# Attention with a bias on one core: reordering the first loads, the first scores and the bias slots

## The chip, the core and the metric

The kernel runs on one core of a Trainium2 chip. The time is the device time of the launch in microseconds (us), the median of several executions. An execution counts as slow when it is over 1.5% above the fastest of the same kernel. A profile, here also called a look, is of one execution. Its span leaves some of the launch out (250.02 us of time had a span of 247.9 us), so spans are compared with spans and times with times. PE is the matmul engine, ACT the one that computes exponentials, DVE the one for elementwise work, POOL the one that issues the loads which convert from f32 to bf16.

## The reference

```
scores = q @ k^T / sqrt(64) + bias          # q, k, v: 4 x 8 x 1024 x 64; bias: 1 x 1 x 1024 x 1024
attn   = exp(scores - max) / (sum(exp(scores - max)) + 1e-8)
out    = attn @ v                            # float32
```

## The kernel before

The 32 heads are worked on in 16 pairs. Scores stand in PSUM with the keys on partitions. The work is cut into 512 banks of 128 keys by 512 queries, three to a *slot*: PE fills a slot's PSUM tile, ACT takes its exponential. There are two such tiles, so a slot's scores can start only when the exponential of the slot two before has ended. exp(bias) is multiplied in afterwards by DVE. It is computed once, in four *bias slots* that use the same PSUM tiles: PE transposes a part of the bias (16 transposes), ACT takes the exponential.

```python
    def s_fill(g):                       # scores of slot g
        ps = ps_s.tile([P, 3, HQ], F32, tag="s", name="ps")
        ...
            nc.tensor.matmul(ps[:, j, :], kT[:, kc, :], qT[:, h, qh * HQ:(qh + 1) * HQ], ...)      # L129
    def s_exp(g):
        nc.scalar.activation(e_at(...), open_ps.pop(("S", g))[:, :n, :], ACTF.Exp, scale=scale)    # L136
    def b_fill(qh, k0):                  # a bias slot: 16 transposes, L144; its exponential is L149
        ps = ps_s.tile([P, 3, 2 * HQ], BF, tag="s", name="pb")...
    ...
        load_qk(1)                       # k and q of pair 1: among the first loads
    ...
        dummy(P)                         # a matmul on zeros, to keep PE busy
        s_fill(0)
        s_exp(0)
        pk1 = k_trans(2, 2, "xa")        # k chunks 2 and 3 of pair 0
        s_fill(1)
        nc.vector.tensor_copy(kT0[:, 2:QC, :], pk1[:])
        nc.vector.memset(vall[:, :, :, D:D1], 1.0)
        s_exp(1)
        pk2 = k_trans(QC, QC, "xb")
        s_fill(2)
        nc.vector.tensor_copy(kT0[:, QC:, :], pk2[:])
        s_exp(2)
        load_v(0)
        nc.gpsimd.dma_start(out=btraw[:, QC:, :], in_=bf_[:, QC:, :])      # second half of the bias
        load_v(1)
        load_qk(2)
```

From slot 3 on the order of every engine's instructions comes from a small simulation when the program is built. It knows a cost for each kind of work (constants such as `MUL = 600` ns) and the times at which loads are expected (`bias_at`, `raw_at`). The result is a fixed order: if PE's next instruction waits, PE waits. The places of the bias slots among the others are set by hand. Transposes of later pairs ("pieces", L89) go through one of two small PSUM buffers, from which DVE copies them (L102 for k, L98 for q).

The softmax here doesn't subtract the row's maximum and nothing guards it: scores larger than these inputs give would overflow.

Of the kernel before, what the change touches and what calls it, by code (L numbers as in the profile page):

```python
# [15 lines left out]
def kernel(  # L16
# [17 lines left out]
    P = 128  # L34
# [37 lines left out]
    def load_qk(pr):  # L72
        qr = raw.tile([P, 2, NCH, D], BF, name="qr")
        kr = raw.tile([P, 2, NCH, D], BF, name="kr")
        nc.gpsimd.dma_start(out=kr.rearrange("p t c d -> p t (c d)"), in_=kf[pr])  # L75
        nc.gpsimd.dma_start(out=qr.rearrange("p t c d -> p t (c d)"), in_=qf[pr])  # L76
        raws[pr] = (qr, kr)

    def load_v(pr):
        for t in range(2):  # L80
            nc.gpsimd.dma_start(out=vall[:, 2 * pr + t, :, :D], in_=vf[pr, :, t])  # L81
# [34 lines left out]
    def e_at(b, n):  # L116
        if b // ET not in etiles:
            etiles[b // ET] = ep.tile([P, ET, HQ], BF, name="E")
        return etiles[b // ET][:, b % ET:b % ET + n, :]
# [3 lines left out]
    def s_fill(g):  # L123
        ps = ps_s.tile([P, 3, HQ], F32, tag="s", name="ps")
        open_ps[("S", g)] = ps
        for j, b in enumerate(slots[g]):
            pr, h, qh, kc = banks[b]
            qT, kT = trs[(pr, 0)], trs[(pr, 1)]
            nc.tensor.matmul(ps[:, j, :], kT[:, kc, :], qT[:, h, qh * HQ:(qh + 1) * HQ],  # L129
                             start=True, stop=b not in late_bias)  # L130
            if b in late_bias:
                nc.tensor.matmul(ps[:, j, :], ident[:], braw[:, late_bias[b], :], start=False, stop=True)

    def s_exp(g):
        n = len(slots[g])
        nc.scalar.activation(e_at(slots[g][0], n), open_ps.pop(("S", g))[:, :n, :], ACTF.Exp, scale=scale)  # L136
# [14 lines left out]
    def mul_pair(b, n=2):  # L151
        pr, h, qh, kc = banks[b]
        e = e_at(b, n)
        if n == 1 or banks[b + 1][1] == h:
            nc.vector.tensor_tensor(e, e, eb[:, qh, kc:kc + n, :], op=ALU.mult)  # L155
        elif n == 4:
            e = e.rearrange("p (c t) q -> p c t q", t=2)
            nc.vector.tensor_tensor(e, e, eb[:, qh, kc:kc + 2, :].unsqueeze(2).to_broadcast([P, 2, 2, HQ]),  # L158
                                    op=ALU.mult)
        else:  # L160
            nc.vector.tensor_tensor(e, e, eb[:, qh, kc:kc + 1, :].to_broadcast([P, n, HQ]), op=ALU.mult)  # L161
# [76 lines left out]
    with tc.manual_schedule():  # L238
# [21 lines left out]
        for x in range(2):  # L260
            for y in range(2):
                nc.vector.memset(mask[x * D:(x + 1) * D, y, :], 1.0 if x == y else 0.0)
        load_qk(1)

        wm = ps_s.tile([P, 3, HQ], F32, tag="s", name="wm")

        def dummy(n):
            nc.tensor.matmul(wm[:, 0, :n], zeros[:, :P], zeros[:, :n], start=True, stop=True)  # L268
# [5 lines left out]
        def k_trans(c0, n, tag):  # L274
            px = ps_x.tile([P, n, P], BF, tag=tag, name="px")
            for c in range(n):
                for t in range(2):
                    nc.tensor.transpose(px[t * D:(t + 1) * D, c, :], kr0[:, t, c0 + c, :], ident[:])
            return px
# [18 lines left out]
            "p b (c q) -> p (b c) q", q=P)[:, :QC, :])  # L298
        q_out(1, pq1)
        nc.scalar.copy(kr0[:, :, 2:QC, :], k0f[:, :, 2:, :])  # L300
        dummy(P)
        s_fill(0)
        s_exp(0)
        pk1 = k_trans(2, 2, "xa")
        s_fill(1)
        nc.vector.tensor_copy(kT0[:, 2:QC, :], pk1[:])
        nc.vector.memset(vall[:, :, :, D:D1], 1.0)
        s_exp(1)
# [3 lines left out]
        s_exp(2)  # L312
        load_v(0)
        nc.gpsimd.dma_start(out=btraw[:, QC:, :], in_=bf_[:, QC:, :])
        load_v(1)
        load_qk(2)

# [3 lines left out]
        EXP, EXP0, QK, AV, TP = 427, 45, 216, 170, 350  # L321
        MUL, COPYQ, COPYK, EVAC, SEM = 600, 650, 420, 620, 80
        order = [("S", g) for g in range(3, NS)]
        for at, x in ((4, (0, 0)), (6, (0, 4)), (10, (1, 0)), (12, (1, 4))):
            order.insert(at, ("B",) + x)
        NO = len(order)
        T0 = 7000.0
        t_act, t_pe, t_dve = T0 + 1400, T0, T0 + 300
        filled = []
        act_end = []  # L330
        x_free = {"xa": T0 - 500, "xb": T0 + 200}
        x_unit = {}
        bias_at = [13000, 21500]
        raw_at = {0: (5900, 7000), 1: (15500, 16500), 2: (26000, 28500)}
        pieces = [(0, 0, 1)]
        for pr in range(1, NP):
            pieces += [(pr, 1, 0), (pr, 0, 0), (pr, 1, 1), (pr, 0, 1)]
# [1 line left out]
        pieces.append((NP, 0, 0))  # L339
        raw_at[NP] = (T0, T0)  # L340
        piece_end = {(0, 1, 0): T0, (0, 0, 0): T0, (0, 1, 1): T0 + 200}
        eb_at = {}
        exp_at = {x: T0 + (0 if x < 3 else 1400) for x in range(6)}
        mul_at = {}
# [14 lines left out]
        ends = {NB - 6: 1, NB - 5: 2, NB - 3: 1}  # L359

        def pe_cost(t, c):
            return c * 2 if t < COLD else c
# [5 lines left out]
        def act_end_of(i):  # L368
            if i < 0:
                return T0  # L370
            if i < len(act_end):
# [162 lines left out]
        def dve_pick():  # L534
            nonlocal mul_next
            c = list(dve_q)
            if mul_next < NB and mul_next not in late_bias:
                pr, h, qh, kc = banks[mul_next]
                b = mul_next
                n = ends.get(b, 2)  # L540
                if b + n - 1 in exp_at and (qh, kc) in eb_at:
                    ready = max(exp_at[b + n - 1], eb_at[(qh, kc)]) + SEM

                    if n == 2 and b % 4 == 0 and b + 3 in exp_at and (qh, kc + 1) in eb_at and b + 3 not in late_bias and \
                            exp_at[b + 3] + SEM <= max(t_dve, ready) and \
                            all(x[0] > max(t_dve, ready) + MUL for x in dve_q):
                        n = 4
                    cost = MUL * n // 2 - 70 * (n // 4)

                    def run(t):  # L550
                        nonlocal mul_next
                        mul_pair(b, n)
                        for x in range(n):
                            mul_at[b + x] = t + cost
                        mul_next += n
                    c.append((ready, 2, cost, run))
            if not c:
                return None
            return min(c, key=lambda x: (max(x[0], t_dve + 100), x[1]))
# [7 lines left out]
        while len(act_end) < NO or av_next < NA or any(last_left) or dve_q:  # L567
            c = []
            a, d, p = act_pick(), dve_pick(), pe_pick()
            if a:  # L570
                c.append((a[0], 0))
# [8 lines left out]
            if who == 0:  # L580
                i = a[2]
                item = order[i]
                t_act = t + a[1]
# [11 lines left out]
            elif who == 1:  # L595
                if d in dve_q:
                    dve_q.remove(d)
                t_dve = t + d[2]
                d[3](t)
            else:  # L600
                t_pe = t + pe_cost(t, p[1])
# [31 lines left out]
```

## Time and profile before

| | before |
|---|---|
| time, median | 250.89 us (3 runs), later 250.74 (6 runs, 250.30 to 251.31) |
| span of the profile | 248.6 us |
| slot 2's exponential starts | 8.37 us |
| second bias half lands | 23.03 us |
| third bias exponential starts | 24.32 us |
| ACT's last exponential ends | 243.83 us |

The third row marks where ACT's row begins to be full, the last where it ends; after it come 4.7 us of last matmuls, division and store. The lines behind this table stand in the prediction.

### The profile page before, as it was taken

What the parts mean: (1) busy time and instruction counts of PE and PEld (TensorE: products, weight loads), DVE (VectorE), ACT (ScalarE), POOL (GpSimd) and SP (SyncE); (2) the same over time, 40 slices, a digit from 0 to 9 for tenths busy, and PEclk for the clock granted to TensorE, in tenths of its full rate; (3) what the DMA queues carried; (4) which work ended last, traced back from release to release, by engine and by line L of the source; (5) the groups of instructions that cost most, each with busy time, mean ns of one, the idle gap of its engine ahead of it and who ended that gap; (6) DMA issues with size and microseconds to landing.
All of it is one profiled execution on the core that took longest, in us unless ns stands there. A gap on an engine that the chain in (4) does not pass through costs nothing.

```text
span 248.6 us, 7122 instructions
## 1 busy us (share of the span) xinstructions
PE 227.5 (92%) x3098; PEld 141.5 (57%) x3153; DVE 219.1 (88%) x377; ACT 240.0 (97%) x183; POOL 53.6 (22%) x74
## 2 busy tenths in 40 slices
PE   7778899999999999999999999999999999999893
PEld 3255656555666656656556556566565555665552
DVE  5228899999999999999999999999999999998884
ACT  4899999999999999999999999999999999999993
POOL 8652413360130221302213055016000000000000
PEclk9999999999999999999999999999999999999998
DMA  5999999599193493921925769629911102020111
GB/s 115 193 197 190 192 132 147 55 148 165 45 154 61 87 119 85 98 87 27 181 44 97 83 87 176 80 87 111 110 38 42 46 0 88 3 84 3 48 60 65
DMA packets 48175, 23.79 MB, mean 96 GB/s; under 512 B 34448, under 2 KB 44048, under 8 KB 47888
## 3 DMA queue, kind: packets, MB, share of 16 engines
q0 software_dynamic: 42272, 14.42, 53.7%
q1 hardware_dynamic: 5584, 8.72, 9.8%
q8 instruction: 24, 0.39, 0.6%
q10 hardware_dynamic: 288, 0.20, 0.3%
q14 instruction: 7, 0.06, 0.1%
HBM read 29.36 MB, written 8.39 MB: 152 GB/s over the span
## 4 chain that ended last, share of the span: by engine, by line
ACT 73%; PE 13%; DMA 5%; DVE 5%; issue 2%; POOL 1%; ACTq 0%
ACT E L136 71%; PE ps L129 8%; DMA btraw<-in_bias_dram 5%; PE px L89 2%; ACT eb L149 1%; PE po L186 1%; DVE E L155 1%; PE wm L268 1%; DVE E L161 1%; DVE E L158 1%; POOL vall L81 1%; DVE qT L98 1%; PE pb L144 0%; PE po L219 0%; DVE oall L198 0%
## 5 line engine op out<-in xcount | busy, mean ns | idle before, releaser
L136 ACT ACTIVATE E<-ps 128x1536 bf16<-128x1536 f32 (+2 forms) x172 | 230.1, 1682 | 1.5 <-PE ps L129 1.4
L129 PE MATMUL ps<-qT,kT 128*128 128x512 bf16 x457 | 135.2, 379 | 12.1 <-ACT E L136 5.4
L186 PEld LDWEIGHTS <-E 128*128 128x128 bf16 x2016 | 82.0, 97 | 37.6 <-DVE E L158 1.6
L158 DVE TENSOR_TENSOR E<-E,eb 128x2048 bf16<-128x2048 bf16 x82 | 98.8, 1216 | 1.1 <-ACT E L136 0.7
L186 PE MATMUL po<-vall,E 128*128 128x65 bf16 x2016 | 91.4, 194 | 1.2 <-DVE E L158 0.5
L129 PEld LDWEIGHTS <-kT 128*128 128x128 bf16 x512 | 45.3, 96 | 43.3 <-issue 8.6
L161 DVE TENSOR_TENSOR E<-E,eb 128x1024 bf16<-128x1024 bf16 x84 | 55.7, 683 | 6.3 <-ACT eb L149 5.2
L75 POOL DMA_DIRECT2D kr<-in_k_dram x15 | 10.5, 700 | 94.6 <-PE px L89 92.7
L81 POOL DMA_DIRECT2D vall<-in_v_dram x32 | 28.1, 883 | 6.6 <-DMA btraw<-in_bias_dram 4.2
L198 DVE TENSOR_TENSOR oall<-po,rs 128x256 f32<-128x256 f32 x63 | 26.7, 424 | 2.3
L98 DVE TENSOR_TENSOR qT<-px,mask 128x1024 bf16<-128x1024 bf16 x31 | 21.3, 687 | 5.6 <-PE px L89 5.0
L102 DVE COPY kT<-px 128x512 bf16<-128x512 bf16 x30 | 12.6, 421 | 2.4 <-PE px L89 1.9
L76 POOL DMA_DIRECT2D qr<-in_q_dram x15 | 10.8, 717 | 18.1 <-PE px L89 16.8
L196 DVE RECIPROCAL rs<-po 128x4 f32<-128x4 f32 x63 | 11.1, 177 | 3.8 <-PE po L186 3.3
L89 PE MATMUL px<-ident,qr 128*64 128x128 bf16 x248 | 12.8, 225 | 0.1
L89 PE MATMUL px<-ident,kr 128*64 128x128 bf16 x240 | 12.4, 225 | 0.3 <-DVE oall L198 0.3
L89 PEld LDWEIGHTS <-qr 128*64 128x64 bf16 x248 | 7.8, 109 | 8.3 <-issue 7.2
L89 PEld LDWEIGHTS <-kr 128*64 128x64 bf16 x240 | 7.7, 109 | 6.3 <-issue 4.6
L149 ACT ACTIVATE eb<-pb 128x2048 bf16<-128x2048 bf16 x4 | 7.5, 1879 | 0.2 <-PE pb L144 0.2
L144 PE MATMUL pb<-ident,btraw 128*128 128x128 bf16 x64 | 4.6, 226 | 1.9 <-ACT eb L149 0.8
L144 PEld LDWEIGHTS <-btraw 128*128 128x128 bf16 x64 | 4.5, 147 | 2.5 <-issue 1.3
L155 DVE TENSOR_TENSOR E<-E,eb 128x1024 bf16<-128x1024 bf16 (+2 forms) x7 | 4.6, 686 | 0.2 <-ACT E L136 0.2
(44 smaller groups left out, 25.8 us busy)
## 6 DMA issues: line engine op xcount, KB each, us to landing
out_dram<-oall SPq DMA_DIRECT2D x30, 256.0 KB, 2.1
vall<-in_v_dram POOLq DMA_DIRECT2D x32, 128.0 KB, 6.6
kr<-in_k_dram POOLq DMA_DIRECT2D x15, 256.0 KB, 4.0
qr<-in_q_dram POOLq DMA_DIRECT2D x15, 256.0 KB, 6.0
btraw<-in_bias_dram POOLq DMA_DIRECT2D x2, 1024.0 KB, 11.3
out_dram<-oall SPq DMA_DIRECT2D x3, 128.0 KB, 1.7
k0f<-in_k_dram SPq DMA_DIRECT2D x2, 128.0 KB, 2.9
q0f<-in_q_dram ACTq DMA_DIRECT2D x1, 128.0 KB, 2.6
```

What stands on the lines that cost most here:

```text
L76: nc.gpsimd.dma_start(out=qr.rearrange("p t c d -> p t (c d)"), in_=qf[pr])
L81: nc.gpsimd.dma_start(out=vall[:, 2 * pr + t, :, :D], in_=vf[pr, :, t])
L89: nc.tensor.transpose(px[t * D:(t + 1) * D, c, :], src[:, t, half * QC + c, :], ident[:])
L98: nc.vector.tensor_tensor(dst[:, :, half * HQ:(half + 1) * HQ], px.rearrange("p c q -> p (c q)").unsqueeze(1).to_broadcast([P, 2, HQ]), ma ...
L102: nc.vector.tensor_copy(dst[:, half * QC:(half + 1) * QC, :], px[:])
L129: nc.tensor.matmul(ps[:, j, :], kT[:, kc, :], qT[:, h, qh * HQ:(qh + 1) * HQ], start=True, stop=b not in late_bias)
L136: nc.scalar.activation(e_at(slots[g][0], n), open_ps.pop(("S", g))[:, :n, :], ACTF.Exp, scale=scale)
L158: nc.vector.tensor_tensor(e, e, eb[:, qh, kc:kc + 2, :].unsqueeze(2).to_broadcast([P, 2, 2, HQ]), op=ALU.mult)
L161: nc.vector.tensor_tensor(e, e, eb[:, qh, kc:kc + 1, :].to_broadcast([P, n, HQ]), op=ALU.mult)
L186: nc.tensor.matmul(acc[:, i, :], e[:, 0, i * P:(i + 1) * P], vall[:, 2 * pr + h, kc, :], start=(kc == 0 and i == 0), stop=(kc == NCH - 1), ...
L196: nc.vector.reciprocal(rs[:], acc[:, :, D:D1])
L198: nc.vector.tensor_tensor(oall[:, c0:c0 + QC, :], acc[:, :, :D], rs[:].to_broadcast([P, QC, D]), op=ALU.mult)
```

## The change

The aim is to have the second bias half on the chip before its slot is due, by loading it and pair 0's V ahead of pair 1's k and q. Pair 1's pieces then come later, so both late bias slots move one place earlier, ahead of pair 1's first slot (slot 11). At the start, slot 1's scores go ahead of four k transposes and a dummy matmul goes. The numbers of the simulation follow.

```diff
-        load_qk(1)                                  # from among the first loads ...
-        dummy(P)
         s_fill(0)
         s_exp(0)
+        s_fill(1)
         pk1 = k_trans(2, 2, "xa")
-        s_fill(1)
...
         nc.gpsimd.dma_start(out=btraw[:, QC:, :], in_=bf_[:, QC:, :])
+        load_qk(1)                                  # ... to behind the second bias half
         load_v(1)
...
-        for at, x in ((4, (0, 0)), (6, (0, 4)), (10, (1, 0)), (12, (1, 4))):
+        for at, x in ((4, (0, 0)), (6, (0, 4)), (9, (1, 0)), (11, (1, 4))):
...
-        T0 = 7000.0
+        T0 = 8000.0                                 # and the starting times that hang on it
-        bias_at = [13000, 21500]
-        raw_at = {0: (5900, 7000), 1: (15500, 16500), 2: (26000, 28500)}
+        bias_at = [13300, 20800]
+        raw_at = {0: (5900, 7800), 1: (22200, 23500), 2: (26000, 28500)}
...
                     cost = MUL * n // 2 - 70 * (n // 4)
+                    if b in ends:
+                        cost = 420 if n == 1 else 690
```

More of the change, by code (lines that the diff above doesn't have):

```diff
@@ L323 @@
         order = [("S", g) for g in range(3, NS)]
-        for at, x in ((4, (0, 0)), (6, (0, 4)), (10, (1, 0)), (12, (1, 4))):
+        for at, x in ((4, (0, 0)), (6, (0, 4)), (9, (1, 0)), (11, (1, 4))):
             order.insert(at, ("B",) + x)
         NO = len(order)
-        T0 = 7000.0
-        t_act, t_pe, t_dve = T0 + 1400, T0, T0 + 300
+        T0 = 8000.0
+        t_act, t_pe, t_dve = T0 + 1400, T0 + 200, T0 + 100
         filled = []
         act_end = []
-        x_free = {"xa": T0 - 500, "xb": T0 + 200}
+        x_free = {"xa": T0 - 500, "xb": T0 + 100}
         x_unit = {}
-        bias_at = [13000, 21500]
-        raw_at = {0: (5900, 7000), 1: (15500, 16500), 2: (26000, 28500)}
+        bias_at = [13300, 20800]
+        raw_at = {0: (5900, 7800), 1: (22200, 23500), 2: (26000, 28500)}
         pieces = [(0, 0, 1)]
```

## The prediction

> **What bounds the kernel now.** I read the page's busy shares first. ACT (ScalarE), which does every exponential, is busy 97% of the span, PE 92% and DVE 88%. Three shares this close decide nothing, so I cut the span at two moments in the timeline: where ACT's third exponential starts (8.37 us) and where its last one ends (243.83 us).
>
> ```profile
> PE 227.5 (92%) x3098; PEld 141.5 (57%) x3153; DVE 219.1 (88%) x377; ACT 240.0 (97%) x183; POOL 53.6 (22%) x74
> ...
> 5.92:8.37 2.45, 2.45 (x18) 0.85 (x19) 0.89 (x3) 1.62 (x2) 0.40 (x2) 1.00 1.17 189
> 8.37:243.83 235.46, 219.67 (x3039) 137.84 (x3094) 213.78 (x359) 235.25 (x174) 48.04 (x61) 1.00 0.65 95
> 243.83:248.60 4.77, 0.86 (x26) 0.73 (x24) 1.20 (x6) 0.52 (x3) 0.00 (x0) 0.75 0.18 57
> ```
>
> The row of a stretch gives its limits, its length, then the busy time of PE, weight loads, DVE, ACT, POOL. In the middle stretch ACT is busy 235.25 of 235.46 us: the time is 8.37 us of start, one unbroken queue of exponentials, and 4.77 us of end. Nothing that PE, DVE or a DMA does in the middle can shorten it, except by removing ACT's idle time. So the next view is what ACT waits for between 5 and 246 us.
>
> ```profile
> ACT E L136 <- PE ps L129: 1.4, 2, 0.7
> ACT oh L232 <- DVE rh L228: 0.8, 1, 0.8
> ACT eb L149 <- PE pb L144: 0.2, 1, 0.2
> ```
>
> Columns: total, times, longest. Two waits of together 1.4 us for the first scores, one of 0.2 us for a bias transpose (L144), and one in the closing stretch. The chain of waits shows what is behind the 0.2 us: the second half of the bias, which lands at 23.03.
>
> ```profile
> 8.03 1.76 POOL vall L81 x2
> 9.79 13.24 DMA btraw<-in_bias_dram
> 23.03 0.05 issue
> 23.08 1.22 PE pb L144 x16
> 24.30 0.02 issue
> 24.32 1.88 ACT eb L149
> ```
>
> Columns: start, length, what. The first waits show in the timeline of PE and of ACT.
>
> ```profile
> 4.91 0.29 PE L268 MATMUL wm<-zeros 128*128 128x128 bf16 x1
> 5.31 0.58 PE L129 MATMUL ps<-qT,kT 128*128 128x512 bf16 x1
> 5.82 0.42 PE L278 MATMUL px<-ident,kr 128*64 128x128 bf16 x4
> 6.17 1.03 PE L129 MATMUL ps<-qT,kT 128*128 128x512 bf16 x2
> 7.14 0.45 PE L278 MATMUL px<-ident,kr 128*64 128x128 bf16 x8
> ...
> 5.92 0.60 ACT L136 ACTIVATE E<-ps 128x512 bf16<-128x512 f32 x1 [0.67 <-PE ps L129]
> 7.24 7.95 ACT L136 ACTIVATE E<-ps 128x1024 bf16<-128x1024 f32 x6 [0.72 <-PE ps L129]
> ```
>
> Slot 0's scores start at 5.31, then come four k transposes, then slot 1's scores at 6.17. ACT has slot 0 done at 6.52 and idles until 7.24. Slot 2's exponential starts at 8.37 where slot 1's would have let it start at about 8.16, so it also waits a little for its scores.
>
> **What the Trainium skill says.** "Perfetto Trace Analysis", section Identifying the Most-Contended Engine, calls matmul busy share a bad measure and occupancy fine for the other engines. The trace agrees: PE's 92% goes with no wait of ACT in the middle. "ScalarE: Activation LUTs", section What ACT_TABLE_LOAD costs, puts ACTIVATE at one element per cycle and lane at 1.2 GHz, so 1536 elements are 1.28 us plus a fixed part. The chain has nine exponentials in 12.03 us, 1.337 each, which agrees: the exponentials' own time is not touched by this change. "DMA: Bandwidth & Descriptors", section Queues, rings and completion order, says that each ring is consumed in order. The completion records of this trace agree for the loads issued on POOL. They land in the order of issue: first bias half 13.23, pair 1's k 14.65 and q 15.91, pair 0's V 17.00 and 17.98, second bias half 23.03. "TensorE: Matmul & The Clock Gate", part 1, says that PE runs at half clock until a free-running window of about 3.4 us was busy. Here transposes last 0.314 us until 5.9 us and 0.219 from 7.3 us on.
>
> **The change part by part.**
>
> (a) *The one dummy matmul before slot 0's scores goes.* It ran 4.91 to 5.20. PE's semaphore record shows its sequencer held from 4.81 to 5.24, until that matmul had completed (5.21), since the scores reuse its PSUM buffer. Without it the scores need only kT, copied at 4.955. Slot 0's scores should start at about 5.04, a gain of 0.26, and its exponential at 5.66.
>
> (b) *Slot 1's scores before the four late k transposes.* They need the second q copy, done at 5.45, so they start at about 5.55. Two matmuls at half clock: the second starts 0.43 later and completes about 0.6 after that, at 6.6. Slot 1's exponential then starts at 6.6 instead of 7.24: ACT's second wait shrinks from 0.72 to about 0.4. But this is not the gain. Slot 2 needs the transposes that were put back: they start at 6.5, complete at 6.95, their copy (0.29) ends at 7.27, slot 2's scores start at 7.33 instead of 7.51 and take the same 0.83, so slot 2's exponential starts at 8.19 instead of 8.37. What is won on slot 1 mostly becomes a longer wait in front of slot 2. **Net for (a) and (b): 0.18 us.**
>
> (c) *Loads.* Before the second bias half stand k and q of pair 1, 1.42 + 1.26 = 2.68 us by the landings above. Moved behind it, they let V land at about 14.3 and 15.3 and the bias half at 23.03 - 2.68 = 20.35. V earlier is worth nothing by itself, since ACT does not wait for the value matmuls. The bias half removes the wait before the third bias exponential. On ends of consecutive exponentials, whose normal distance is 1.77 us for a bias slot, that one came 0.31 us late (the view's 0.2 is start to end, overlaps left out). The new slot order takes that exponential one slot (1.34 us) earlier: its transposes may begin after slot 8 ends, about 21.1, still 0.7 after the landing. **Gain 0.31 us.**
>
> (d) *The price of (c).* Pair 1's k lands at 20.35 + 1.42 = 21.8 and q at 23.0 instead of 14.65 and 15.91. Slot 11 holds the first bank of pair 1. Moved behind the last bias slot, it should start at about 27.4: the third bias exponential comes 24.32 - 8.37 - 0.31 - 1.34 = 14.30 us after slot 2's (without the late 0.31 and with one score slot fewer between), so at 8.19 + 14.30 = 22.5, and then one bias, one score and one bias slot follow, 1.77 + 1.34 + 1.77. So its scores (0.81) must start by 26.4. From q's landing at 23.0 come transposes (0.41) and a DVE copy (0.69), done by 24.3 plus what they wait behind DVE's multiplies (1.21 each): 25.5 at worst. A second of slack, so **0 us**, but the thinnest margin of the change.
>
> (e) *Costs of the last multiplies in the schedule's model* (420 and 690 ns; the tail shows 419 and 681 to 693). This only reorders instructions at the end. After the last exponential come 26 matmuls, the division and the store. DVE's last multiply ends at 243.97 there and the last matmul at 244.68; a better order may save some tenths or nothing: **0.05 us**. The new starting times of the model shift the static order everywhere else, beside a full ACT.
>
> Sum: 0.18 + 0.31 + 0.05 = 0.54, or 250.35 from 250.89.
>
> **The rivals.**
>
> *A wait takes the place of the one removed.* Pair 1's pieces need a PSUM buffer, which value matmuls now also use at that time, and queue behind DVE's multiplies. If (d) is a microsecond too tight, ACT stalls before slot 11 by up to 1 us and the result is 250.9 to 251.4. For: all four pieces come within five microseconds in which DVE also starts on the second bias half. Against: DVE idled 5.2 us before the first bias exponential and 1.5 us near 24 us, and the order of slots was changed to give them time.
>
> *The start gains more, or loses.* If PE reaches full clock before slot 2's transposes, slot 2 comes earlier and the whole 0.6 of slot 1 counts: 249.9. If the removed dummy or the phase of the window delays the full clock past slot 2's scores, three matmuls at 0.43 instead of 0.216 cost 0.6: 250.9. The window is free-running, so single runs may differ.
>
> *The transfer is hidden anyway.* Then only the start counts, 250.7. Against it: the 0.31 us is in ACT's own row.
>
> *PE or DVE becomes the bound* by an unlucky order: ACT's 0.2 us of idle in 235 says that this schedule has room, so I give it little.
>
> **Range and chances.** The mean of these, with (d) failing a little one time in five, is 250.3. The runs before spread over 0.7 us (250.61 to 251.31), as large as the effect, so the range is 249.6 to 251.1. Two per cent is 5 us; no wait of that size exists that the change could remove, since ACT's work alone is 237 us. Faster 0.01, within 2% 0.97, slower 0.02.
>
> **What would show it.** Right: no dummy before slot 0, its scores near 5.04; ACT's waits for scores still about 1.4 in total or more, with slot 2 at about 8.2; the second bias half landing near 20.4 and no wait of ACT for L144; slot 11 without a wait; the middle stretch of ACT about 0.3 shorter. Wrong: a wait of ACT near 27 us for scores, with PE waiting for a qT or kT copy of pair 1; a full clock that comes later than 7.3 us; a middle stretch with idle ACT elsewhere, meaning the new static order hurts; or a tail that changes by more than 0.3 us.

## The result, and the profile after

The changed kernel takes 250.14 us in the median of 6 runs (249.60 to 251.05), the kernel before in the same rounds 250.74. The ratio is 0.9979, 95% interval 0.9957 to 1.0001. Ratios here are the mean time of one kernel's fast runs over that of the other's fast runs of the same rounds, so not quite the ratio of the medians.

First the span cut at the same two places as before: from slot 2's exponential (7.79) to the end of the last (243.21). The columns after the length are the busy times of PE, weight loads, DVE, ACT, POOL.

```profile
7.78:243.21 235.43, 220.50 (x3044) 137.13 (x3096) 213.80 (x355) 235.29 (x174) 49.92 (x63) 1.00 0.65 96
243.21:247.90 4.69, 0.79 (x20) 0.61 (x18) 1.24 (x6) 0.53 (x3) 0.00 (x0) 0.75 0.18 58
```

The middle is 235.43 us long and full, against 235.46 before: it did not become shorter. The end is as before. So all of the 0.62 us by which the last exponential ends earlier (243.83 to 243.21) is in the start. Second, what ACT waited for between 5 and 246 us:

```profile
ACT oh L232 <- DVE rh L228: 0.8, 1, 0.8
ACT E L136 <- PE ps L129: 0.8, 3, 0.3
```

The wait for the bias transposes (L144) is gone from this list, and the waits for scores fell from 1.4 to 0.8 us. Third, the timeline of PE and of ACT at the start:

```profile
4.95 1.47 PE L129 MATMUL ps<-qT,kT 128*128 128x512 bf16 x3
6.35 0.63 PE L277 MATMUL px<-ident,kr 128*64 128x128 bf16 x12
6.91 1.27 PE L129 MATMUL ps<-qT,kT 128*128 128x512 bf16 x5
...
6.45 1.02 ACT L136 ACTIVATE E<-ps 128x1024 bf16<-128x1024 f32 x1 [0.26 <-PE ps L129]
7.79 2.79 ACT L136 ACTIVATE E<-ps 128x1536 bf16<-128x1536 f32 x2 [0.31 <-PE ps L129]
```

The scores of slots 0 and 1 run in one piece from 4.95, then twelve transposes, then slot 2. By the trace's completion records the second bias half landed at 19.57, pair 1's k at 20.85 and its q at 22.49. So why is the middle not shorter? The chain of waits at the last two bias slots answers that:

```profile
22.35 0.69 PE ps L129 x3
23.04 0.36 PE px L89 x8
23.40 0.02 issue
23.42 0.43 DVE kT L102
23.86 0.04 issue
23.90 0.41 PE px L89 x8
24.31 1.15 PE pb L144 x16
25.47 0.02 issue
25.49 1.88 ACT eb L149
```

In front of the fourth bias slot's transposes stand pair 1's q transposes, and they wait for a DVE copy of pair 1's k, which itself came late. ACT's own timeline shows the size:

```profile
22.14 1.88 ACT L149 ACTIVATE eb<-pb 128x2048 bf16<-128x2048 bf16 x1
23.91 1.44 ACT L136 ACTIVATE E<-ps 128x1536 bf16<-128x1536 f32 x1
25.49 1.88 ACT L149 ACTIVATE eb<-pb 128x2048 bf16<-128x2048 bf16 x1
```

Slot 10 ends at 23.91 + 1.44 = 25.35 and the bias slot at 25.49 + 1.88 = 27.37, 2.02 us later. Such a slot that is fed in time ends 1.77 us after the one before it, so this one is late: 0.24 us by the trace's nanoseconds. Reckoned in the same way, the third bias slot is 0.07 late. In front of its transposes PE's timeline has four value matmuls, which waited for a multiply of DVE:

```profile
20.81 0.29 PE L186 MATMUL po<-vall,E 128*128 128x65 bf16 x4 [0.46 <-DVE E L158]
20.94 1.16 PE L144 MATMUL pb<-ident,btraw 128*128 128x128 bf16 x16
```

Slot 8's exponential, which frees the PSUM tile, had ended at 20.84. No run took these matmuls away, so the cause of the 0.07 is read from the order and not shown. Together the two make the 0.31 us that the earlier landing had won. The view of waits does not list it, because the start of an exponential overlaps the end of the one before: read ends, not idle time, when tenths matter.

### The profile page after: what moved, and what is told of

The parts are those of the page before. It is cut to its first block, busy times and chain, and to the rows that moved or that the text cites. A ratio compares the mean times of both kernels' runs of the same rounds, so it can differ in the third digit from the quotient of the medians.

```text
span 247.9 us, 7112 instructions
## 1 busy us (share of the span) xinstructions
PE 227.8 (92%) x3098; PEld 140.6 (57%) x3152; DVE 218.6 (88%) x371; ACT 240.1 (97%) x183; POOL 53.7 (22%) x74
## 4 chain that ended last, share of the span: by engine, by line
ACT 84%; PE 9%; DVE 3%; issue 2%; ACTq 0%
ACT E L136 81%; PE ps L129 5%; ACT eb L149 2%; PE po L186 1%; DVE E L155 1%; PE wm L267 1%; DVE E L158 1%; PE pb L144 1%; PE px L89 1%; DVE kT L102 0%; DVE oall L198 0%; PE px L277 0%; DVE qT L98 0%; PE px L282 0%; ACT kT L295 0%
## 5 line engine op out<-in xcount | busy, mean ns | idle before, releaser
L158 DVE TENSOR_TENSOR E<-E,eb 128x2048 bf16<-128x2048 bf16 x88 | 106.2, 1217 | 7.3 <-ACT eb L149 6.0
L161 DVE TENSOR_TENSOR E<-E,eb 128x1024 bf16<-128x1024 bf16 x72 | 47.8, 683 | 0.9 <-ACT E L136 0.7
L144 PE MATMUL pb<-ident,btraw 128*128 128x128 bf16 x64 | 4.7, 226 | 1.5 <-ACT eb L149 1.0
L144 PEld LDWEIGHTS <-btraw 128*128 128x128 bf16 x64 | 4.4, 147 | 2.3 <-issue 1.2
```

Of the source, the lines that this page charges most:

```text
L144: nc.tensor.transpose(ps[:, j, i * P:(i + 1) * P], btraw[:, qh * QC + i, :].rearrange("p (kp kc) -> p kc kp", kc=NCH)[:, k0 + j, :], ident[:])
L158: nc.vector.tensor_tensor(e, e, eb[:, qh, kc:kc + 2, :].unsqueeze(2).to_broadcast([P, 2, 2, HQ]), op=ALU.mult)
L161: nc.vector.tensor_tensor(e, e, eb[:, qh, kc:kc + 1, :].to_broadcast([P, n, HQ]), op=ALU.mult)
```

## The experiments

Two questions were open: where the 0.59 us at the start came from, and whether the lost 0.31 us has the cause that the chain suggests. The looks are compared in a table at the end of this section; its "middle" is the stretch from the end of slot 2's exponential to the end of the last.

**1. The start alone.** The first theory: in the kernel before, an earlier start is worth nothing, since the third bias slot stands at 24.3 us whatever happens.

```diff
 kernel before
-        dummy(P)
         s_fill(0)
         s_exp(0)
-        pk1 = k_trans(2, 2, "xa")
         s_fill(1)
+        pk1 = k_trans(2, 2, "xa")
```

> The kernel before with the two edits of the start alone (no dummy matmul before slot 0's scores; slot 1's scores ahead of the late k transposes); loads and slots as before. Theory: the start's gain is lost again at the third bias exponential, because its transposes cannot begin before the second bias half lands, near 23.0 us as in the kernel before. So slot 2's exponential starts 0.2 to 0.6 us earlier than 8.37, the third bias exponential still starts near 24.3, ACT's last exponential ends near 243.8, and the time is that of the kernel before (ratio 0.999 to 1.001). Rival: gains add up, the start is worth its 0.6 by itself, the last exponential ends near 243.2, ratio 0.9977.

Measured: slot 2's exponential started at 7.28, 1.09 us earlier than before. The chain of waits and ACT's waits between 5 and 246 us:

```profile
9.80 13.25 DMA btraw<-in_bias_dram
23.04 0.05 issue
23.09 1.20 PE pb L144 x16
24.29 0.02 issue
24.31 1.88 ACT eb L149
...
ACT eb L149 <- PE pb L144: 1.1, 1, 1.1
```

The bias exponential starts at 24.31 as in the kernel before (24.32), the wait in front of it grew to 1.1 us, and the last exponential ended at 243.82 (before: 243.83). In this execution the whole 1.09 us was given back, 0.20 of it already at the first bias slot, whose half of the bias had landed at 12.91, and the rest here. The timed ratio is 0.9982 (0.9965 to 0.9999), a little better than the theory's 0.999. Run 8 shows why that may be: in executions with a late start the bias is not what is waited for, and there the start's edits count.

**2. The loads alone,** the start as before; the moved slots and the new numbers of the simulation stay in.

```diff
 changed kernel
+        dummy(P)
         s_fill(0)
         s_exp(0)
+        pk1 = k_trans(2, 2, "xa")
         s_fill(1)
-        pk1 = k_trans(2, 2, "xa")
```

> The changed kernel with the start of before put back (dummy matmul, k transposes ahead of slot 1's scores); loads, slots and model numbers as changed. Theory: the wait for the second bias half is gone, but the fourth bias slot comes late by about as much (0.2 to 0.3 us) because PE stands behind pair 1's q transposes, which wait for a DVE copy; slot 2 starts near 8.4, the last exponential ends near 243.8, ratio 0.999 to 1.001. Rival (the prediction's own sum): 0.31 us gained, last exponential near 243.5, ratio 0.9988.

Measured: no wait for the second bias half, but the third bias slot 0.09 and the fourth 0.21 us late, 0.30 together, as in the changed kernel. Slot 2 started at 7.98 and the last exponential ended at 243.40, earlier than the theory's 243.8, because of the start; the middle is what the theory said. Timed: 251.05 us, ratio 1.0003 (0.9977 to 1.0029).

**3. Truer landing times in the simulation.** Its 22.2 and 23.5 us for pair 1's k and q are 1.35 and 1.0 us later than they landed (20.85, 22.49), so the simulation places the k transposes behind slot 10's scores, when they could stand in front.

```diff
 changed kernel
-        raw_at = {0: (5900, 7800), 1: (22200, 23500), 2: (26000, 28500)}
+        raw_at = {0: (5900, 7800), 1: (21000, 22700), 2: (26000, 28500)}
```

> The changed kernel with pair 1's landing times in the schedule's model set to 21.0 and 22.7 us, near the 20.85 and 22.49 that its trace shows, in place of 22.2 and 23.5: the static order then has pair 1's k transposes ahead of slot 10's scores. Theory: the late fourth bias slot goes away, ACT loses nothing after slot 2, its last exponential ends 0.3 us earlier than in the changed kernel (near 242.9), ratio to the kernel before 0.9967, that is about 249.9 us. Rival: the lateness comes from PE's or DVE's amount of work there and moves to slot 10 or slot 11, last exponential near 243.2, ratio 0.998.

> The version with truer landing times in the model, once more, now beside the changed kernel on the same chip. Theory: from slot 2's end to ACT's last end 233.8 us, 0.15 to 0.25 less than in the changed kernel, since the fourth bias slot is in time; in the timed runs this is covered by the start's variation unless both have many early starts: ratio to the changed kernel 0.998 to 1.001. Rival: no difference in that stretch either, because the late first bias slot of the last look (0.18) belongs to this order and not to that execution's DMA.

> The version with truer landing times a third time, as the standard for the two with dummy work. From slot 2's end to ACT's last end again 233.8 us, the fourth bias slot in time; ratio to the kernel before 0.9965 to 0.998.

It was run three times. The timelines of PE and ACT of the third:

```profile
22.39 0.41 PE L89 MATMUL px<-ident,kr 128*64 128x128 bf16 x8
22.74 0.82 PE L129 MATMUL ps<-qT,kT 128*128 128x512 bf16 x3
23.49 0.41 PE L89 MATMUL px<-ident,qr 128*64 128x128 bf16 x8
...
24.27 1.45 ACT L136 ACTIVATE E<-ps 128x1536 bf16<-128x1536 f32 x1
25.61 1.89 ACT L149 ACTIVATE eb<-pb 128x2048 bf16<-128x2048 bf16 x1
```

The k transposes now stand ahead of slot 10's scores (22.74), the copy is done under them, and the q transposes find their buffer free. By the trace's nanoseconds the fourth bias slot ends at 27.49, 1.77 us after slot 10 (25.72): in time. That held in all three looks and in both of run 7, which have the same order, while it was 0.21 to 0.24 late in all five looks with the changed kernel's order (three of the changed kernel, runs 2 and 6). The third bias slot kept its 0.07 to 0.10. The middle fell from 234.0 to 233.8. All three last exponentials end later than the 242.9 of the theory, by their late starts (table). In the first look the middle was 233.96, because the first bias half landed at 14.74 instead of 13.0 and the first bias slot was 0.18 late; that did not come back. The mechanism is shown. In time it is small beside the scatter: 250.78, 250.53 and 250.14 us, ratios to the kernel before 0.9978, 0.9976 and 0.9956, where the changed kernel in the same rounds had 0.9989 and 0.9969 beside the last two.

**4. The bias slots back.**

```diff
 changed kernel
-        for at, x in ((4, (0, 0)), (6, (0, 4)), (9, (1, 0)), (11, (1, 4))):
+        for at, x in ((4, (0, 0)), (6, (0, 4)), (10, (1, 0)), (12, (1, 4))):
```

> The changed kernel with the last two bias slots where they were before (positions 10 and 12), so that slot 11, the first of pair 1, comes before the fourth bias slot again. Theory: pair 1's q pieces are then late for slot 11, since q lands at 22.5 and transposes, copy and scores take about 2 us more: ACT waits 0.3 to 0.9 us near 25 us, the last exponential ends near 243.3 to 243.9, ratio 0.998 to 1.0005. Rival: the slots' move is not needed because the pieces are in time; no wait, last exponential near 242.9, ratio 0.9967.

Measured, in ACT's and PE's timeline:

```profile
26.81 1.45 ACT L136 ACTIVATE E<-ps 128x1536 bf16<-128x1536 f32 x1 [0.15 <-PE ps L129]
...
25.61 0.41 PE L89 MATMUL px<-ident,kr 128*64 128x128 bf16 x8 [0.30 <-DVE kT L102]
```

Slot 11 is 0.26 us late, by the same kind of wait: its scores stand behind a piece, the second half of pair 1's k, whose buffer was held until the copy of the first half. So in this order pair 1's pieces are not in time in the old places either; moving the slots moved the lateness from slot 11 to a bias slot and made the middle no shorter (233.95 here, 233.98 in the changed kernel). Whether truer landing times would have been enough in the old places was not run. The size is just under the theory's 0.3 to 0.9; the last exponential ended at 244.55, later than both theories had it, since slot 2 started at 9.15 in this execution. Ratio 0.9980 (0.9962 to 0.9998).

**5. The changed kernel again,** twice, and **6.** with the dummy matmul put back.

> The changed kernel itself, once more. In the traces so far slot 2's exponential started at 7.28 to 9.15 us, and the matmul durations say that PE's full clock came between 4.3 and 10.5 us, in different executions, whatever the kernel. Theory: most of the 0.59 us by which slot 2 was earlier in the first trace of the changed kernel is this clock and not the edit; slot 2's start will differ by several tenths from 7.79 in this one, while everything from slot 2's end to ACT's last end again takes 233.9 to 234.0 us, with the fourth bias slot 0.2 us late. Rival: slot 2 starts at 7.7 to 7.9 again, the gain is the edit's.

> The changed kernel a third time, beside these. From slot 2's end to ACT's last end again 234.0 us (more by what a first bias half that lands late adds); ratio to the kernel before 0.998 to 0.999.

```diff
 changed kernel
+        dummy(P)
         s_fill(0)
```

> The changed kernel with the one dummy matmul put back before slot 0's scores. Theory: slot 0's scores start 0.3 us after the copy of kT ends instead of 0.05, since they wait for the dummy's completion; slot 1's scores need the second q copy anyway, so slot 1 and slot 2 are at most 0.1 later than with the same clock without it. Rival: the dummy keeps PE busy and the full clock comes earlier with it, so slot 2 is earlier.

The three looks at the changed kernel have slot 2 at 7.79, 7.40 and 7.62 and a middle of 233.98, 234.10 and 234.03; the last two contain 0.13 and 0.05 for the first bias slot, whose half landed at 13.0 to 13.1 and which now waits for that landing when the start is early. Timed: 250.54 us (0.9989, 0.9949 to 1.0029) and 250.58 us (0.9969, 0.9928 to 1.0010).

With the dummy back, slot 0's scores started at 5.20, 0.29 us after kT's copy ended (4.91); without it, 0.05 after (4.95 against 4.90). Its wait is as the prediction had it. What it costs slot 2 this look can't say: slot 2 started at 7.99, but k's second half landed at 6.74 in this execution and PE waited 0.35 us for it.

**7. More work for PE at the start.** The looks showed that PE's full clock comes at very different moments (table below). In run 3's second look PE idled 0.49 us before the q transposes and 0.36 before slot 0's scores, and the full clock came at 9.82. The idea was to fill the second gap, and in a second version also the first. A look taken in the same round as these speaks against the idea: in the changed kernel's third PE idled 0.49 and 0.34 us at the same two places, and the full clock came at 5.05. Such gaps alone do not set it.

```diff
 version of run 3
-        dummy(P)
+        for i in range(3):                                   # second version only
+            dummy(P)
 ...
         pq1 = q_trans(1, ...)
+        for i in range(2):                                   # both versions
+            nc.tensor.transpose(pqt[:, 16 + i, :], zeros[:, :P], ident[:])
```

> The version with truer landing times, plus two dummy transposes after the q transposes, written to a part of that PSUM tile which nothing reads, so that PE works where it waits for the copy of kT and the scores don't wait for their completion. Theory: the late full clock (9.0 and 9.8 us in two looks, both with q's landing late and PE idle 0.5 and 0.4 us in front of the transposes and the scores) comes from too little PE work[...]; with the second gap filled the late starts (slot 2 at 9.15) become rarer, the median is 249.8 to 250.3 and the ratio to the kernel before 0.996 to 0.998. Rival: the clock's moment is a matter of chance that two short transposes don't move; ratio as without them, 0.9977.

> The same with two more short dummy matmuls ahead of the first q transposes, where PE waited 0.5 us when q landed late. Theory: late starts go away altogether (no execution with slot 2 at 9.1), but where q lands early the two cost 0.2 us; ratio 0.996 to 0.998, with a smaller spread than the changed kernel's 1.7 us. Rival: the spread stays, and the two only cost their 0.2 us.

The first took 249.76 us (ratio 0.9953, 0.9912 to 0.9994), the lowest median; four of its six spans are 247.6 to 248.0, the others 249.0 and 249.4. The second took 250.78 us (0.9973, 0.9933 to 1.0013), spread 249.70 to 251.29, not narrower. Beside run 3's version in the same rounds (250.14 us, 0.9956) neither can be told from it, so whether such dummies bring the clock forward stays open. In the profiled execution of the first version the first bias half landed at 14.52 and its slot was 0.96 us late; that one look has a span of 249.0 and tells nothing against it.

**8. The kernel before again.**

> The kernel before, once more. Theory: the second bias half lands near 23.0 and the third bias exponential starts near 24.3 whatever the start was; ACT's last exponential ends at 243.8 if slot 2 starts before 8.7, and later by the difference if it starts later. Rival: its end follows its start, earlier or later, as in the changed kernel.

Here slot 2 started at 9.58, there was no wait for the second bias half (landed 22.96), and the last exponential ended at 244.72. As the theory has it: until about 8.7 us (8.37 and the 0.31 lost at the third bias slot) the start does not matter to the kernel before, after it every tenth does.

All looks, in us. The full clock is the first moment at which the trace's clock record grants it. Some ends are a start and a length added as the views print them, and can be 0.01 off.

| look | q transposes start | full clock from | slot 2 starts | last exponential ends | middle |
|---|---|---|---|---|---|
| before | 3.69 | 7.25 | 8.37 | 243.83 | 234.01 |
| before, again | 4.15 | 9.45 | 9.58 | 244.72 | 233.69 |
| start alone | 3.84 | 4.26 | 7.28 | 243.82 | 235.10 |
| loads alone | 3.65 | 6.41 | 7.98 | 243.40 | 233.97 |
| changed | 3.63 | 6.60 | 7.79 | 243.21 | 233.98 |
| changed, 2nd | 3.64 | 4.13 | 7.40 | 242.95 | 234.10 |
| changed, 3rd | 4.15 | 5.05 | 7.62 | 243.10 | 234.03 |
| truer landings, 1st | 4.16 | 9.05 | 9.15 | 244.56 | 233.96 |
| truer landings, 2nd | 4.15 | 9.82 | 9.14 | 244.37 | 233.78 |
| truer landings, 3rd | 3.73 | 7.24 | 8.14 | 243.35 | 233.76 |
| bias slots back | 4.16 | 10.48 | 9.15 | 244.55 | 233.95 |
| dummy back | 3.65 | 5.62 | 7.99 | 243.41 | 233.98 |
| more PE work, first | 3.84 | 6.76 | 8.13 | 244.30 | 234.72 |
| more PE work, second | 3.85 | 5.27 | 7.70 | 242.90 | 233.76 |

The changed kernel and run 3's version have the same instructions up to slot 2. In the third look of the one and the second of the other q was equally late (4.15) and slot 0's scores started at 5.47 both times; slot 2 started at 7.62 and at 9.14, with the full clock at 5.05 and at 9.82. So looks must be paired by the clock. With it at 7.25 and 7.24: old start 8.37, new start 8.14. At 6.41 and 6.60: 7.98 and 7.79. At 9.45 and 9.82, q equally late: 9.58 and 9.14. The edits of the start are worth 0.19 to 0.44 us; the other part of the 0.59 us in the first pair of profiles goes with the clock. Whether the edits themselves move the clock stays open: it came between 4.13 and 10.48 with the new start and between 6.41 and 9.45 in three looks with the old. The transposes show the clock without the record, in PE's and ACT's timelines of the changed kernel's third look and, below the second dots, of run 3's second:

```profile
6.29 0.53 PE L277 MATMUL px<-ident,kr 128*64 128x128 bf16 x12
...
7.62 2.79 ACT L136 ACTIVATE E<-ps 128x1536 bf16<-128x1536 f32 x2 [0.21 <-PE ps L129]
...
6.86 0.85 PE L277 MATMUL px<-ident,kr 128*64 128x128 bf16 x12
...
9.14 1.45 ACT L136 ACTIVATE E<-ps 128x1536 bf16<-128x1536 f32 x1 [1.15 <-PE ps L129]
```

The same twelve transposes take 0.53 us in the one and 0.85 in the other, and slot 2's three score matmuls, which follow, start some 0.23 us apart in the one and 0.40 to 0.43 in the other.

## Why the prediction was right or wrong

The time was forecast at 250.3 and came out at 250.14, inside the range. The sum was right, one of its terms was not, and the terms do not add as the sum has it; that it came out is luck.

- **What bounds the kernel: right.** ACT's row is full from slot 2 to the end in both kernels, and every tenth of the result is found in ACT's idle time or late ends.
- **(a), the dummy: right.** Slot 0's scores start 0.05 us after kT's copy, at 4.95 (forecast 5.04).
- **(b), slot 1 earlier, mostly given back at slot 2: right in kind and, for a like clock, in size.** Forecast 0.18 net; measured 0.19, 0.23 and 0.44 in the three pairs. One detail failed: slot 2's scores were to wait for the copy of the late transposes. They began at 6.91, before that copy ended (7.09), since slot 2's first bank uses an earlier chunk of k. A sign failed too: ACT's waits for scores were to stay near 1.4 us or more and came to 0.8, and to 1.2 in run 3's third look, whose clock is that of the first profile before.
- **(c), 0.31 us from the earlier bias: this step failed.** The landing was earlier by more than forecast (19.57, forecast 20.35) and the wait went. But new waits took its place. At the fourth bias slot it was 0.24: PE stood behind pair 1's q transposes, whose buffer was held until a late copy of k. It was the first rival, at another place than the one it named. Run 3 shows the cause: with the k transposes ahead of slot 10's scores the 0.24 is gone. At the third it was 0.07, behind value matmuls as it seems (not shown).
- **Adding (a), (b) and (c): a second failure.** They are not separate. In the kernel before the third bias slot cannot start before 24.3, so an earlier start is swallowed whole (run 1). What the loads did was to let the start count, not to add 0.31 of their own. This is read from looks; in the times the start alone (0.9982) can't be told from the whole change (0.9979).
- **(d), slot 11: right.** No wait there, and run 4 shows that the margin is thin: in the old places it would be 0.26 late.
- **(e), the end: nothing.** By the nanoseconds there are 4.72 us from the last exponential to the end of the span, before and after. The forecast named some tenths or nothing, and counted 0.05.
- **The rival on the clock was underrated.** It was meant as some tenths either way; with the same start and q equally late, slot 2 moved by 1.52 us, more than the change is worth.

The first profile's 0.62 us is thus about 0.2 from the start's edits, about 0.4 from a clock that came earlier in that execution, and nothing net from the bias wait. But the 0.4 counts only because the loads were moved: in the kernel before an early clock changes nothing (run 1). So what the change is worth depends on the clock. An estimate from the looks, with the kernel before ending at 243.83 unless slot 2 starts after 8.7, as run 8 has it, and the changed kernel's middle of 233.98: at an early clock (run 2's and the changed kernel's first look, 6.41 and 6.60) the gain is 243.83 - 243.21, some 0.6 us; at a late one (9.45 and 9.82) the changed kernel with slot 2 at 9.14 would end at 244.57, where the kernel before ended at 244.72, some 0.15.

Over all timed rounds the changed kernel is 0.1 to 0.3% faster (0.9979, 0.9989, 0.9969), each interval reaching 1: a gain of that size is likely, not proved. Runs 1 and 4, run 3's version in two of three rounds and the first version of run 7 have intervals just below 1; that any of them beats the changed kernel itself is not shown.

## What to carry to other kernels

Where one engine's row is full, savings ahead of a fixed event, such as a load's landing, add nothing until that event moves: look for the latest of the things that a slot waits for before you add up gains. In a fixed instruction order, a wrong guess of when data lands makes an engine stand behind work that could have come earlier, so compare such guesses with the landings in the trace. When a change is worth tenths, pair profiles by whatever differs between executions (here PE's clock at the start) before crediting the edit.

## What the Trainium skill lacked or had wrong

- "TensorE: Matmul & The Clock Gate", part 1, says the ramp varies between runs and costs under 1% of a typical span. The first holds here, and the variation seen is within the second, but the page does not say how busy PE must be for the full clock to come. PE worked from 1.24 us on with gaps of a few tenths, and the full clock came between 4.13 and 10.48 us. Two looks with the same instructions up to slot 2 and nearly the same gaps (0.49 us, then 0.34 and 0.36) got it at 5.05 and 9.82, which moved the first full slot by 1.52 us (7.62 and 9.14): 0.6% of the time and more than the change under study.
- "ScalarE: Activation LUTs", section What ACT_TABLE_LOAD costs, gives an ACTIVATE without pointer operands 186 ns + 0.833 ns per element and an overlap of about 93 ns back to back: for 1536 elements an estimate of 186 + 1280 - 93 = 1373 ns. Nine exponentials in a row took 12.03 us in the kernel before, 1337 ns each, some 3% less.
